# Turning the heads' outputs on VectorE, in 32x32 blocks, and parking them by four transfers

## The chip, the cores and the metric

The kernel runs on one core of a Trainium2 chip. The metric is the device time of one execution in microseconds (us), and it is measured in several runs. The engines of a core are named as in the profile: PE (TensorE's matmuls; PEld its weight loads), DVE (VectorE), ACT (ScalarE), POOL (GpSimd), SP (SyncE, which issues most of the transfers). L1268 is line 1268 of the kernel.

## The reference

One layer of a hybrid block: a normalised and modulated input goes through one projection, three groups of heads work on it, each output passes a gate, and one output projection adds it to the residual. The part that matters here is the normalisation of a head's output and its gate, cut from the reference:

```python
def from_heads(t):
    b, h, l, d = t.shape
    return t.transpose(0, 2, 1, 3).reshape(b, l, h * d)

def head_out(o, w, z):
    o = o * lax.rsqrt(jnp.mean(o * o, axis=-1, keepdims=True) + NORM_EPS) * w.astype(jnp.float32)
    return from_heads(o).astype(z.dtype) * jax.nn.silu(z)
...
    y_l = head_out(o_lf + flip_seq(o_lb), norm_w, z_l)
```

There are 512 latent tokens, a model width of 2048 and heads of 128: six gated-DeltaNet heads, six mLSTM heads, and 512 channels of long convolutions (Hyena).

## The kernel before

The input projection streams its weights in tiles of 128 x 512. Each is split into an upper and a lower half of the mantissa (`whi` by ACT, `wlo` by DVE, lines 275 and 276), and a product is three matmuls (lines 418, 419, 423; 421, 422, 425 for the context). That stream is the fill of the program: wherever nothing else is due, the next weight tiles stand.

Beside it run chains: the DeltaNet heads (`gdn`, one after another), the mLSTM scans (`ml_scans`), a row of gates, and four long convolutions (`convs`). A planner, `weave`, decides the order in which the program is written down: each chain yields a pair (cost on PE, latency), in units of its own, and is called again when its latency is over; the fill takes the rest. A list scheduler then fixes the order of instructions on each engine from that. The engines work in that order, and wait for each other by semaphores. A helper, `paced`, ties an instruction to the stream's matmul planned just before it (line 423), so that it does not run ahead.

A head ends in `head_norm` (line 1254, called 12 times). Its output `osb` has tokens on the partitions (4 pieces of 128 tokens) and the 128 channels of the head along each row. DVE takes the root mean square and scales it. Then `head_norm` yields a latency `LN` of 20, PE turns the four pieces by transposes into a PSUM bank (L1268), ACT copies the bank to the tile `yo` (L1270), and POOL issues one transfer of 256 KB (L1271) that parks it in `yraw` in DRAM, with channels as rows. `yo` has one buffer, shared with a tile of the heads' preparation (`qsq`, L1318) and one of the inversion.

The output projection is worked in four blocks of 512 columns. The first, `first_cols`, is the end of the fill. For each k of its 16 operands it calls `y_operand` (L1733): ACT issues the load of the gate `zt` (L1736), POOL that of the parked output `yr` (L1743), and DVE multiplies the two and the norm's weight (L1744; for four of the k's, the convolutions', L1741 does it without a parked output). The product is split into `yh` and `yl` (lines 275 and 276), and `y_product` makes the twelve matmuls (three by four tokens' pieces, L1762 to L1764). The long convolutions that are still to be done at that time share DVE, ACT, POOL and PE with it: four products `tt` with the spectrum `hs` (L1674 to L1677) in each of four frequency steps, two additions on POOL (L1679, L1680), the split `O`, and matmuls back (L323 to L325, and the ends, L1696 to L1700).

Of the kernel before, what the change touches and what calls it, by code (L numbers as in the profile page):

```python
# [10 lines left out]
F32 = mybir.dt.float32  # L11
# [3 lines left out]
AF = mybir.ActivationFunctionType  # L15
ALU = mybir.AluOpType
# [4 lines left out]
SEQ = 512  # L21
# [4 lines left out]
NL = SEQ // 128  # L26
# [3 lines left out]
EPS = 1e-6  # L30
# [194 lines left out]
def block_kernel(ctx: ExitStack, tc: tile.TileContext, io, out, dbg=None):  # L225
    nc = tc.nc
    PE, ACT, DVE, POOL, SP = nc.tensor, nc.scalar, nc.vector, nc.gpsimd, nc.sync
# [12 lines left out]
    def bank(tag, bufs, name=None):  # L240
        return ps.tile([128, 512], F32, tag=tag, bufs=bufs, name=name or tag)
# [26 lines left out]
    ident = const.tile([128, 128], F32, name="ident")  # L268
# [127 lines left out]
    yraw = dr.tile([KT, 128, SEQ], F32, name="yraw")  # L396
# [7 lines left out]
    def paced(ins):  # L404


        if stream[0] is not None:
            together(ins, [stream[0]])
# [51 lines left out]
    with ExitStack() as st:  # L460
# [23 lines left out]
        for k in range(KT):  # L484
# [11 lines left out]
            t = x_slot(F32)  # L496
# [27 lines left out]
        p = p_s()  # L524
        PE.matmul(p, w1, featsT, start=True, stop=True)
        h1 = sin_layer(p, 0)
        p = p_s()
# [86 lines left out]
        for k in range(KT):  # L614
# [6 lines left out]
            with tc.high_priority():  # L621
                for g in range(4):
                    G_ = slice(32 * g, 32 * g + 32)
                    i = PE.matmul(pa[G_], ones[:, 0:32], sqs[g], start=f, stop=l, tile_position=(0, 32 * g))
# [5 lines left out]
        pt = p_ml()  # L630
# [261 lines left out]
    with ExitStack() as st:  # L892
# [17 lines left out]
        for t0, n in ((0, 4), (4, 2)):  # L910
            pt = p_s()
# [339 lines left out]
        DVE.tensor_copy(MF[1][B, :, A], pv[B])  # L1251
        yield 1.0, LL

    def head_norm(o_sb, eps_ap, eps_imm, ss, kt_out, bank):

        v = s1.tile([128, NL], F32, tag="hn_v", bufs=2, name="hn_v")
        if eps_ap is not None:
            DVE.scalar_tensor_tensor(out=v, in0=ss, scalar=1.0 / 128, in1=eps_ap, op0=ALU.mult, op1=ALU.add)
        else:
            DVE.tensor_scalar(out=v, in0=ss, scalar1=1.0 / 128, scalar2=eps_imm, op0=ALU.mult, op1=ALU.add)  # L1260
        r = s1.tile([128, NL], F32, tag="hn_r", bufs=2, name="hn_r")
        rsqrt(s1, r, v, [128, NL], "rsq", 4)
        for t in range(NL):
            DVE.tensor_single_scalar(out=o_sb[:, t], in_=o_sb[:, t], scalar=r[:, t:t + 1], op=ALU.mult)
        yield 0, LN
        pt = bank()
        for t in range(NL):
            PE.transpose(pt[:, 128 * t:128 * t + 128], o_sb[:, t], ident)  # L1268
        yo = s1.tile([128, SEQ], F32, tag="yo", bufs=1, name="yo")
        ACT.activation(out=yo, in_=pt, func=AF.Copy)  # L1270
        POOL.dma_start(out=yraw[kt_out], in_=yo)  # L1271
        yield 0.6, 0.0

    def gdn_prep(h, kT, vT, qT):

# [91 lines left out]
    def gdn_scan(h, kT, qT, kt, vr, dd, eq, AT, MF):  # L1367
# [53 lines left out]
            S = s  # L1421
        if h == 0:
            dump("o_gdn", o_sb.rearrange("p t c -> p (t c)"))
        yield from head_norm(o_sb, eq, None, ss, h, p_st)

    def z_tile(k):

# [36 lines left out]
    def ml_scan(h, kT, vT, qT, oT):  # L1464
# [82 lines left out]
        junk = s1.tile([128, 128], F32, tag="junk", bufs=1, name="junk")  # L1547
        for j in range(NL):
            ACT.activation(out=junk, in_=o_sb[:, j], func=AF.Square, accum_out=ss[:, j:j + 1])
        yield from head_norm(o_sb, None, 4.0 * EPS, ss, 10 + h, p_s)  # L1550

    def residual_gate():

# [179 lines left out]
    def y_operand(k, pool):  # L1733

        zt = yt[0].tile([128, SEQ], F32, tag="zt", bufs=2, name="zt3")
        ACT.dma_start(out=zt, in_=zd[k])  # L1736
        w = hnw[:, 0:1] if k < 6 else hnw[:, 2:3] if k < 10 else hnw[:, 1:2]
        yr = yt[0].tile([128, SEQ], F32, tag="yr", bufs=2, name="yr3")
        if 6 <= k < 10:
            assert (1, (k - 6) // 2) in hdone  # L1740
            DVE.scalar_tensor_tensor(out=yr, in0=yv[k - 6], scalar=w, in1=zt, op0=ALU.mult, op1=ALU.mult)  # L1741
        else:
            POOL.dma_start(out=yr, in_=yraw[k])  # L1743
            DVE.scalar_tensor_tensor(out=yr, in0=yr, scalar=w, in1=zt, op0=ALU.mult, op1=ALU.mult)  # L1744
        yh[k] = pool.tile([128, SEQ], F32R, tag="y", bufs=KT, name="yh")
        yl[k] = pool.tile([128, SEQ], F32R, tag="y", bufs=KT, name="yl")
        split_hi_lo(yh[k], yl[k], yr)
# [124 lines left out]
```

## Time and profile before

| | us |
|---|---|
| median of three runs | 1501.56 (1501.19 to 1502.5) |
| profiled execution, own time | 1500.16 |
| its span | 1498.4 |
| PE busy | 1450.9 (97%) |
| DVE busy | 1033.0 (69%) |
| ACT busy | 572.6 (38%) |
| POOL busy | 217.0 (14%) |

The profiled execution is one execution; the span runs from its first instruction to its last. The busy times of engines overlap. PE's mean clock was 0.997 of full speed. A group of instructions is those of one line, engine and form of tile; its idle time is what the engine waited just before them.

### The profile page before, as it was taken

How to read it: one execution, taken by the hardware profiler on the slowest of the kernel's cores; microseconds unless marked ns; L12 is line 12 of the kernel's file. 1: busy time of each engine (PE TensorE's matmuls, PEld its weight loads, DVE VectorE, ACT ScalarE, POOL GpSimd, SP SyncE). 2: the span in 40 equal slices, each digit the busy share in tenths (PEclk: the TensorE clock that was granted, in tenths of full speed). 3: DMA queues.
4: the chain of work that ended last, by engine and by line, in shares of the span. 5: the costliest groups of instructions: out<-in, count | busy, mean ns of one | idle time of the engine just before them, and what ended most of it. 6: DMA issues, size and time to landing. Idle time of an engine off the chain costs nothing.

```text
span 1498.4 us, 25081 instructions
## 1 busy us (share of the span) xinstructions
PE 1450.9 (97%) x8822; PEld 1187.8 (79%) x8822; DVE 1033.0 (69%) x2685; ACT 572.6 (38%) x1367; POOL 217.0 (14%) x412
## 2 busy tenths in 40 slices
PE   5999999999999999999999999999999999999997
PEld 1566678888888888878887888888878888888785
DVE  4666777577868787867776776677675676774553
ACT  5443344425242524262435333533353333333431
POOL 2224002111110211021102101200011121210000
PEclk9999999999999999999999999999999999999999
DMA  9998623333244323442344223311322542465543
GB/s 316 318 320 289 224 74 106 95 105 114 85 138 117 120 93 117 127 125 92 120 117 132 85 71 93 114 57 57 86 79 81 166 169 92 143 231 154 163 129 102
DMA packets 145237, 202.82 MB, mean 135 GB/s; under 512 B 57222, under 2 KB 57703, under 8 KB 144856
## 3 DMA queue, kind: packets, MB, share of 16 engines
q1 hardware_dynamic: 89752, 159.50, 33.0%
q0 software_dynamic: 10048, 32.52, 6.9%
q10 hardware_dynamic: 45312, 9.21, 3.2%
q8 instruction: 69, 1.13, 0.3%
q14 instruction: 56, 0.46, 0.1%
HBM read 182.92 MB, written 18.26 MB: 134 GB/s over the span
## 4 chain that ended last, share of the span: by engine, by line
PE 80%; DVE 7%; DMA 5%; issue 3%; ACT 2%; POOL 1%; SPq 0%; ACTq 0%; DVEq 0%; POOLq 0%
PE ml L418 14%; PE ml L419 13%; PE ml L423 13%; PE mc L422 3%; PE mc L421 3%; PE mc L425 3%; PE st L317 2%; DVE wlo L276 2%; PE st L1764 1%; PE st L1763 1%; PE st L1762 1%; PE st L1386 1%; PE st L1395 1%; PE st L1379 1%; PE st L1508 1%
## 5 line engine op out<-in xcount | busy, mean ns | idle before, releaser
L418 PE MATMUL ml<-xh,whi 128*128 128x512 f32 x1024 | 423.1, 413 | 0.0
L419 PE MATMUL ml<-xs,whi 128*128 128x512 f32 x1024 | 407.1, 398 | 0.0
L423 PE MATMUL ml<-xh,wlo 128*128 128x512 f32 x1024 | 404.5, 395 | 0.0
L275 ACT ACTIVATE whi<-raw 128x512 fp32r<-128x512 f32 x320 | 200.9, 629 | 488.3 <-PE mc L422 165.4
L276 DVE TENSOR_TENSOR wlo<-raw,whi 128x512 fp32r<-128x512 f32 x320 | 222.2, 696 | 175.9 <-ACT whi L275 171.8
L418 PEld LDWEIGHTS ml<-xh,whi 128*128 128x128 f32 x1024 | 193.4, 189 | 33.8 <-issue 1.7
L423 PEld LDWEIGHTS ml<-xh,wlo 128*128 128x128 f32 x1024 | 192.7, 188 | 24.9
L419 PEld LDWEIGHTS ml<-xs,whi 128*128 128x128 f32 x1024 | 193.6, 189 | 18.9
L421 PE MATMUL mc<-cs,whi 128*128 128x256 f32 x384 | 110.4, 288 | 0.0
L422 PE MATMUL mc<-cs,whi 128*128 128x256 f32 x384 | 108.7, 283 | 0.0
L425 PE MATMUL mc<-cs,wlo 128*128 128x256 f32 x384 | 107.8, 281 | 0.0
L422 PEld LDWEIGHTS mc<-cs,whi 128*128 128x128 f32 x384 | 72.3, 188 | 16.0
L421 PEld LDWEIGHTS mc<-cs,whi 128*128 128x128 f32 x384 | 72.1, 188 | 15.6
L425 PEld LDWEIGHTS mc<-cs,wlo 128*128 128x128 f32 x384 | 73.4, 191 | 0.0
L1564 DVE SCALAR_TENSOR_TENSOR gacc<-mg,scol,gacc 128x512 f32<-128x512 f32 x60 | 45.0, 749 | 25.7 <-DMA mg<-in_mg_dram 17.4
L1281 POOL DMA_DIRECT2D G<-rows_d x36 | 19.8, 553 | 223.0 <-DVE T L1147 76.0
L1271 POOL DMA_DIRECT2D yraw<-yo x12 | 7.1, 589 | 293.2 <-ACT yo L1270 218.1
L1506 POOL TENSOR_SCALAR ke<-kt,wend 128x128 f32<-128x128 f32 x60 | 27.0, 452 | 87.5 <-PE st L1508 43.9
L1333 ACT ACTIVATE ex<-G,ngc 128x128 f32<-128x128 f32 x72 | 26.8, 397 | 32.4 <-DVE M L1335 10.9
L1763 PE MATMUL st<-wlo,yh 128*128 128x512 f32 x96 | 37.7, 392 | 0.0
L1764 PE MATMUL st<-whi,yl 128*128 128x512 f32 x96 | 37.7, 392 | 0.0
L1762 PE MATMUL st<-whi,yh 128*128 128x512 f32 x96 | 37.6, 391 | 0.0
(501 smaller groups left out, 2877.4 us busy)
## 6 DMA issues: line engine op xcount, KB each, us to landing
raw<-in_wt_dram SPq DMA_DIRECT2D x256, 256.0 KB, 2.8
mw<-in_mw_dram SPq DMA_DIRECT2D x128, 256.0 KB, 5.9
mg<-in_mg_dram SPq DMA_DIRECT2D x64, 256.0 KB, 2.7
raw<-in_wo_dram SPq DMA_DIRECT2D x64, 256.0 KB, 2.9
fraw<-in_wf_dram SPq DMA_DIRECT2D x16, 320.0 KB, 5.4
G<-rows_d POOLq DMA_DIRECT2D x36, 128.0 KB, 3.3
xs<-in_xT_dram SPq DMA_DIRECT2D x16, 256.0 KB, 5.9
hspec<-hv POOLq DMA_DIRECT2D x16, 256.0 KB, 5.7
```

The lines of the kernel that those rows point to most:

```text
L275: ACT.activation(out=hi, in_=src, func=AF.Copy)
L276: DVE.tensor_tensor(out=lo, in0=src, in1=hi.bitcast(F32), op=ALU.subtract)
L418: PE.matmul(pl[:m], wh, xh[:, kk], start=f, stop=False)
L419: PE.matmul(pl[:m], wh, xl[kk], start=False, stop=False)
L421: PE.matmul(pc[:m, :CTX], wh, ch[kk], start=f, stop=False)
L422: PE.matmul(pc[:m, :CTX], wh, cl[kk], start=False, stop=False)
L423: stream[0] = PE.matmul(pl[:m], wl, xh[:, kk], start=False, stop=l)
L425: PE.matmul(pc[:m, :CTX], wl, ch[kk], start=False, stop=l)
L1564: paced(DVE.scalar_tensor_tensor(out=acc, in0=m, scalar=sk, in1=acc, op0=ALU.mult, op1=ALU.add))
L1762: PE.matmul(o, yh[k][:, ts_], wh, start=f, stop=False)
L1763: PE.matmul(o, yh[k][:, ts_], wl, start=False, stop=False)
L1764: PE.matmul(o, yl[k][:, ts_], wh, start=False, stop=l)
```

## The change

`head_norm` no longer takes a bank. In place of the transposes, the copy and the one transfer, DVE turns the output in square blocks of 32 x 32, in one instruction, from `osb` to `yo`, which is now laid out as 128 partitions x 4 x 4 x 32. The blocks themselves stay where they were; so four transfers, issued by ACT and each `paced`, move 32 partitions (64 KB) each to their place in `yraw`, in runs of 512 bytes. The chain yields a cost of 0 and a latency of 2.5 after the turning and 0 at the end, where it yielded 0.6 after the transposes.

Within a row of `yraw` the tokens now stand in another order, by blocks. `y_operand` loads the parked output into a new tile, `pk`, with one buffer, and makes the product in four instructions of 128 columns, each of which reads its blocks from `pk` by strides and writes `yr` in the old order. The load is still POOL's.

```diff
-    def head_norm(o_sb, eps_ap, eps_imm, ss, kt_out, bank):
+    def head_norm(o_sb, eps_ap, eps_imm, ss, kt_out):
...
         yield 0, LN
-        pt = bank()
-        for t in range(NL):
-            PE.transpose(pt[:, 128 * t:128 * t + 128], o_sb[:, t], ident)
-        yo = s1.tile([128, SEQ], F32, tag="yo", bufs=1, name="yo")
-        ACT.activation(out=yo, in_=pt, func=AF.Copy)
-        POOL.dma_start(out=yraw[kt_out], in_=yo)
-        yield 0.6, 0.0
+        yo = s1.tile([128, 4, NL, 32], F32, tag="yo", bufs=1, name="yo")
+        DVE.transpose(out=yo.rearrange("p g t j -> p t g j"), in_=o_sb.rearrange("p t (g j) -> p t g j", j=32))
+        yield 0, 2.5
+
+        for q, Q in enumerate(QS):
+            paced(ACT.dma_start(out=yraw[kt_out].rearrange("(a i) (q x) -> q i a x", a=4, q=4)[q],
+                                in_=yo[Q].rearrange("i a t j -> i a (t j)")))
+        yield 0, 0.0
...
         else:
-            POOL.dma_start(out=yr, in_=yraw[k])
-            DVE.scalar_tensor_tensor(out=yr, in0=yr, scalar=w, in1=zt, op0=ALU.mult, op1=ALU.mult)
+            pk = yt[0].tile([128, SEQ], F32, tag="pk", bufs=1, name="pk")
+            POOL.dma_start(out=pk, in_=yraw[k])
+            for t in range(NL):
+                ts_ = slice(128 * t, 128 * t + 128)
+                DVE.scalar_tensor_tensor(out=yr[:, ts_].rearrange("p (q j) -> p q j", q=4), scalar=w, op0=ALU.mult,
+                                         op1=ALU.mult, in0=pk.rearrange("p (q t j) -> p t q j", t=NL, q=4)[:, t],
+                                         in1=zt[:, ts_].rearrange("p (q j) -> p q j", q=4))
```

The two calls of `head_norm` drop their last argument. Below L1266 a line of the kernel after stands one lower than before, and from L1745 on six lower.

What this does to the order of the engines is shown at three places. The first is DVE in the first columns of the output projection, at two frequency steps of a convolution: `tt` and `O` are the convolution's, `yr`, `yl` the gate's product and its lower half, `wlo` the lower half of a weight. Before:

```order
L276 TENSOR_TENSOR O<-tt,O 128x256
L1744 SCALAR_TENSOR_TENSOR yr_14716<-yr_14716,hnw,zt_14714 128x512
L276 TENSOR_TENSOR O<-tt,O 128x256
L276 TENSOR_TENSOR wlo<-raw,whi 128x512
L276 TENSOR_TENSOR yl<-yr_14716,yh 128x512
L1674 TENSOR_TENSOR tt<-st,hs 128x256
L1675 SCALAR_TENSOR_TENSOR tt<-st,c_alt,hs 128x256
L1676 TENSOR_TENSOR tt<-st,hs 128x256
L1677 SCALAR_TENSOR_TENSOR tt<-st,c_alt,hs 128x256
```

And after, in that stage:

```order
L276 TENSOR_TENSOR O<-tt,O 128x256
L1748 SCALAR_TENSOR_TENSOR yr_14441<-pk,hnw,zt_14439 128x128
L276 TENSOR_TENSOR wlo<-raw,whi 128x512
L276 TENSOR_TENSOR O<-tt,O 128x256
L1748 SCALAR_TENSOR_TENSOR yr_14441<-pk,hnw,zt_14439 128x128 x3
L1645 TENSOR_TENSOR eo<-hy 128x256
L1675 TENSOR_TENSOR tt<-st,hs 128x256
L1676 SCALAR_TENSOR_TENSOR tt<-st,c_alt,hs 128x256
L1677 TENSOR_TENSOR tt<-st,hs 128x256
L1678 SCALAR_TENSOR_TENSOR tt<-st,c_alt,hs 128x256
L276 TENSOR_TENSOR yl<-yr_14441,yh 128x512
```

One product has become four, spread around the convolution's work. `eo`, the first fold of a convolution, has moved into this place, since a second convolution now lies here; before, only the last did.

The second place is POOL in the same stage: loads of the parked outputs between additions of the convolution. Before:

```order
L1743 DMA yr_14716<-yraw 128x512
L1743 DMA yr_14767<-yraw 128x512
L1679 TENSOR_TENSOR tt<-tt 128x256
L1680 TENSOR_TENSOR tt<-tt 128x256
L1743 DMA yr_14827<-yraw 128x512
L1679 TENSOR_TENSOR tt<-tt 128x256
L1680 TENSOR_TENSOR tt<-tt 128x256
```

And after:

```order
L1745 DMA pk<-yraw 128x512
L1680 TENSOR_TENSOR tt<-tt 128x256
L1681 TENSOR_TENSOR tt<-tt 128x256
L1680 TENSOR_TENSOR tt<-tt 128x256
L1681 TENSOR_TENSOR tt<-tt 128x256
L1745 DMA pk<-yraw 128x512 x4
L1680 TENSOR_TENSOR tt<-tt 128x256
L1681 TENSOR_TENSOR tt<-tt 128x256
```

The four loads in a row go to the one buffer, each behind the products that read the one before, and they stand ahead of the next additions.

The third place is ACT at the end of a head: `yo` is the head's output, `whi` the upper half of a weight, `kT`, `tanh` and `qT` the next head's. Before:

```order
L1082 ACTIVATE tanh<-kT 128x256
L1270 ACTIVATE yo<-s 128x512
L275 ACTIVATE whi<-raw 128x512
L1082 ACTIVATE tanh<-kT 128x512
L275 ACTIVATE whi<-raw 128x512 x2
L1069 ACTIVATE qT<-ml,gcw 128x512
```

And after:

```order
L1082 ACTIVATE tanh<-kT 128x512
L1271 DMA yraw<-yo 32x4x128 x2
L275 ACTIVATE whi<-raw 128x512
L1271 DMA yraw<-yo 32x4x128 x2
L275 ACTIVATE whi<-raw 128x512
L1069 ACTIVATE qT<-ml,gcw 128x512
```

The copy has gone, and the four issues stand in pairs around a weight's half.

## Rows read from the trace of the kernel before

**Rows 1.** The page's first part (busy time of each engine, share of the span, instructions) and, from its fourth part, the chain that ended last by engine.

```profile
PE 1450.9 (97%) x8822; PEld 1187.8 (79%) x8822; DVE 1033.0 (69%) x2685; ACT 572.6 (38%) x1367; POOL 217.0 (14%) x412
...
PE 80%; DVE 7%; DMA 5%; issue 3%; ACT 2%; POOL 1%; SPq 0%; ACTq 0%; DVEq 0%; POOLq 0%
```

**Rows 2.** All instructions of line 1268 on PE, the transposes of the heads' outputs: engine, operation, names, count; shortest, median and longest in ns; first and last start.

```profile
L1268 PE MATMUL s<-ident,osb x24: 270/272/330, 376.9 to 1142.5; 128*128 128x128 f32 x24
...
L1268 PE MATMUL st<-ident,osb x24: 270/272/273, 417.2 to 1189.3; 128*128 128x128 f32 x24
```

**Rows 3.** The timeline of PE around the first head's transposes: start in us, duration in us, then line and names; the transposes share one row (x4).

```profile
376.63 0.39 PE L423 MATMUL ml<-xh,wlo 128*128 128x512 f32 x1
376.86 0.60 PE L1268 MATMUL s<-ident,osb 128*128 128x128 f32 x4
377.22 0.48 PE L418 MATMUL ml<-xh,whi 128*128 128x512 f32 x1
377.54 0.39 PE L419 MATMUL ml<-xs,whi 128*128 128x512 f32 x1
```

**Rows 4.** Groups of instructions by line and form on ACT and POOL, the last from the page: busy us and mean ns of one, then idle time ahead of them and what ended it. The weights' upper halves, the copies of the heads' outputs from PSUM, and the issues that park them.

```profile
L275 ACT ACTIVATE whi<-raw 128x512 fp32r<-128x512 f32 x320 | 200.9, 629 | 488.3 <-PE mc L422 165.4 <-PE ml L419 156.7 <-issue 30.2
...
L1270 ACT ACTIVATE yo<-st 128x512 f32<-128x512 f32 x6 | 3.6, 598 | 10.8 <-PE st L1268 10.8
...
L1270 ACT ACTIVATE yo<-s 128x512 f32<-128x512 f32 x6 | 3.5, 590 | 0.6 <-PE s L1268 0.5
...
L1271 POOL DMA_DIRECT2D yraw<-yo x12 | 7.1, 589 | 293.2 <-ACT yo L1270 218.1
```

**Rows 5.** Groups by line and form on DVE, columns as in rows 4: the gate's product, a product of a quarter of its size, and block transposes of two sizes.

```profile
L1744 DVE SCALAR_TENSOR_TENSOR yr<-yr,hnw,zt 128x512 f32<-128x512 f32 x12 | 8.9, 745 | 2.3 <-DMA yr<-yraw 2.3
...
L1534 DVE SCALAR_TENSOR_TENSOR osb<-nm,dn,osb 128x128 f32<-128x128 f32 x24 | 8.4, 351 | 0.8
...
L1184 DVE STREAM_TRANSPOSE L<-U 128x384 f32<-128x384 f32 x6 | 3.4, 571 | 0.2
...
L1101 DVE STREAM_TRANSPOSE Mb<-Mc 128x192 f32<-128x192 f32 x6 | 2.3, 378 | 0.6 <-ACT Mc L1099 0.4
```

**Rows 6.** Two stretches of the span: its length, then the busy time and count of instructions of PE, PEld, DVE, ACT and POOL, PE's granted clock, the DMA share and GB/s. The second is the stretch from the first products of the output columns to the end of the last convolution.

```profile
1200.00:1292.80 92.80, 91.69 (x537) 80.21 (x537) 68.33 (x138) 28.42 (x60) 18.53 (x24) 1.00 0.37 121
1292.80:1334.50 41.70, 40.68 (x221) 34.18 (x220) 34.19 (x64) 17.31 (x34) 12.19 (x19) 1.00 0.62 192
```

**Rows 7.** The timeline of DVE in that second stretch: start in us, duration in us, line and names, and in brackets the idle time ahead with what ended it.

```profile
1305.16 0.49 DVE L276 TENSOR_TENSOR O<-tt,O 128x256 fp32r<-128x256 f32 x1 [0.65 <-ACT O L275]
1305.58 0.74 DVE L1744 SCALAR_TENSOR_TENSOR yr<-yr,hnw,zt 128x512 f32<-128x512 f32 x1
1306.24 0.41 DVE L276 TENSOR_TENSOR O<-tt,O 128x256 fp32r<-128x256 f32 x1
1306.58 0.68 DVE L276 TENSOR_TENSOR wlo<-raw,whi 128x512 fp32r<-128x512 f32 x1
1307.18 0.68 DVE L276 TENSOR_TENSOR yl<-yr,yh 128x512 fp32r<-128x512 f32 x1
1307.78 0.41 DVE L1674 TENSOR_TENSOR tt<-st,hs 128x256 f32<-128x256 f32 x1
...
1308.84 0.47 DVE L1677 SCALAR_TENSOR_TENSOR tt<-st,c_alt,hs 128x256 f32<-128x256 f32 x1
...
1331.38 0.42 DVE L1696 TENSOR_TENSOR cv<-st,bs 128x256 f32<-128x256 f32 x1
...
1332.05 0.68 DVE L276 TENSOR_TENSOR wlo<-raw,whi 128x512 fp32r<-128x512 f32 x1
1332.65 0.74 DVE L1698 SCALAR_TENSOR_TENSOR cv<-hy,c_skip,cv 128x512 f32<-128x512 f32 x1
1333.31 0.68 DVE L276 TENSOR_TENSOR yl<-yr,yh 128x512 fp32r<-128x512 f32 x1
```

**Rows 8.** The timeline of PE, in the same stretch: five starts of the output columns' matmuls (512 wide) lie from the first row to the second, and eight of the convolution's (256 wide) from the second to the third.

```profile
1317.71 0.39 PE L1763 MATMUL ml<-wlo,yh 128*128 128x512 f32 x1
...
1318.86 0.28 PE L323 MATMUL st<-iv,O 128*128 128x256 f32 x1
...
1319.80 0.28 PE L325 MATMUL st<-iv,O 128*128 128x256 f32 x1
```

**Rows 9.** Issues of transfers: the z tiles on ACT, and the read-back of the parked outputs on POOL, each with its shortest, median and longest issue in ns, and the read-back's time to landing in us.

```profile
L1736 ACTq DMA_DIRECT2D zt<-zd x16: 326/327/350, 1168.6 to 1340.9; - x16
...
L1743 POOL DMA_DIRECT2D yr<-yraw x12: 538/555/597, 1159.2 to 1330.5; - x12
...
DMA to landing us min/median/max: 2.9/3.1/4.3
```

**Rows 10.** The waits of the whole span: who waited for whom; total us, times, longest us.

```profile
DVE O L276 <- ACT O L275: 9.2, 15, 1.1
...
PE s L1478 <- ACT kt L1479: 6.7, 4, 2.7
...
DVE tt L1674 <- DMA hs<-hspec: 2.5, 4, 1.0
```

**Rows 11.** Two stretches of the head stage, columns as in rows 6.

```profile
640.00:660.00 20.00, 17.62 (x103) 14.29 (x102) 12.26 (x34) 14.04 (x39) 7.79 (x16) 1.00 0.49 150
780.00:800.00 20.00, 17.51 (x85) 14.27 (x83) 15.14 (x27) 4.72 (x9) 1.90 (x4) 1.00 0.51 144
```

More of the change, by code (lines that the diff above doesn't have):

```diff
@@ L1423, in gdn_scan @@
             dump("o_gdn", o_sb.rearrange("p t c -> p (t c)"))
-        yield from head_norm(o_sb, eq, None, ss, h, p_st)
+        yield from head_norm(o_sb, eq, None, ss, h)
     def z_tile(k):
@@ L1549, in ml_scan @@
             ACT.activation(out=junk, in_=o_sb[:, j], func=AF.Square, accum_out=ss[:, j:j + 1])
-        yield from head_norm(o_sb, None, 4.0 * EPS, ss, 10 + h, p_s)
+        yield from head_norm(o_sb, None, 4.0 * EPS, ss, 10 + h)
     def residual_gate():
```

## The prediction

> **What bounds the kernel now.** I read the shares of the engines first, then the groups of the lines that the change touches, then the stage in which the gate's products are made. TensorE (PE) is busy for 1450.9 of 1498.4 us, and the chain that ended last is 80% PE, 7% VectorE (DVE), 5% DMA [rows 1]. So PE time that goes is time that goes, wherever PE is full; work added to DVE, ScalarE (ACT) or GpSimd (POOL) costs only where PE comes to wait for it. The place to look for that is the stretch in which the output projection's first columns run together with the last long convolution: there DVE is busy for 34.19 of 41.70 us while PE is still nearly full (40.68) [rows 6]. Just before, it is 68.33 of 92.80. That stretch is the only one, of those the change touches, where DVE and PE stand so close.
>
> **What goes from PE.** Each of the 12 heads' outputs has four transposes on PE, 48 in all, at 272 ns each [rows 2]. Their durations overlap, so the price is the gap they make in the stream: after the matmul of 376.63 the four start at 376.86, the next matmul at 377.22, and the one behind it not until 377.54 [rows 3]. From 376.63 to 377.54 are 0.91 us, for two steps that take 0.23 us each in a full stream (376.63 to 376.86, or 1.15 us for five [rows 8]): 0.91 - 0.46 = 0.45 us a head, 12 x 0.45 = 5.4 us. The bounds are 12 x 0.36 (only 376.86 to 377.22) = 4.3 and 48 x 0.272 = 13.1 us. I take 5.4, read from the place itself; nearly all of these heads lie where PE is full, so I count all of it as gain.
>
> A rule of the Trainium skill speaks against this part: "VectorE: DVE Perf Modes", section "Rules for kernel authors", says to make a 128x128 transpose on TensorE if a PSUM destination will do, and VectorE's only for 32x32 blocks. The row at 376.86 agrees that TensorE's is cheap, 0.45 us for four; by that rule the most that this part can give is the 5.4 us above.
>
> **What goes from and comes to the others in the head stage.** ACT loses 12 copies of 0.59 us = 7.1 us, POOL 12 issues of 0.59 us = 7.1 us [rows 4]. DVE gains 12 block transposes of 128x512. The trace has 571 ns for 128x384 and 378 ns for 128x192, 1.0 ns a column, so 0.70 us (bounds: 0.57, the wide row itself, and 1.1, twice that row) and 8.4 us in all [rows 5]. ACT gains 48 issues of transfers; its issues of the z tiles, which have the nearest row, take 0.327 us: 15.7 us [rows 9]. Neither is on the path by itself: ACT is busy 38% and DVE 69% of the span [rows 1], and PE's weight tiles hide it. If that cover were gone, the 8.4 us would come on top. Each issue is tied to the product planned just before it (the last matmul of a weight tile, line 423), so ACT waits there for PE; queued behind it are the rounding of the next weights' halves, for which DVE waits and then PE. The issues stand in ACT's order between the weight halves (two, a half, two more), so each pair holds a half up by 0.65 us, while ACT sat idle 488 us before these halves, 165 of it until PE [rows 4]: it is early, and I count the wait at nothing. What waits for the parked data is far behind: a head's output is read back only in the last stage.
>
> What may change in the head stage is how a head's end collides with its neighbours. PE loses time there in some 20-us windows: the two worst show 17.62 and 17.51 us busy of 20 [rows 11]; the wait for the copies of the mLSTM's keys makes 6.7 us of it [rows 10]. The change keeps the chain of heads waiting for longer (a planner cost of 2.5 in place of 0.6), so heads, scans and fill interleave anew, and ACT's order of those copies against the inversion's load changes for heads 2 to 5. I take 0 for it, between -6.7 (all of those waits go) and +5 (two more such windows).
>
> **The gate's product.** The one product of 128x512 (745 ns) is split in four of 128x128; the nearest row of that size is 351 ns [rows 5]. By start to start, the large one is 0.66 us (1305.58 to 1306.24 [rows 7]); the difference of the durations is 394 ns, so a small one starts 0.66 - 0.39 = 0.27 us behind the last. Four are 1.08 us, 0.42 us more for each k. Bounds: 0 (the elements are as many) and 4 x 0.351 - 0.745 = 0.66 us. Twelve k's give 5.0 us more on DVE, ten of them, 4.2 us, in the busy stretch.
>
> The Trainium skill says in "Perfetto Trace Analysis", section "Optimizing Scalar/DVE Operations", that each instruction pays a fixed access overhead and that small ones should be joined where the engine is saturated; the rows agree in direction, 351 ns for a quarter of the elements of a 745 ns one.
>
> The order adds more to that stretch. The convolution (1,0) used to run inside the input projection's tiles; now both (1,0) and (1,1) lie among the first 132 matmuls of the output columns, with ten k's. Counted in the new order of DVE, from the first yl of that stage to the end of the last convolution, by start-to-start times of [rows 7]: 13 yl and 11 wlo at 0.60 = 14.4; 40 small products at 0.27 = 10.8; 2 large ones at 0.66 = 1.3; 8 frequency steps, four tt each (1.46) = 11.7; 16 O at 0.38 = 6.1; 4 folds at 0.34 = 1.4; 2 el at 0.60 = 1.2; 4 ends of a convolution (0.67 + 0.66 + 0.60) = 7.7. Sum 54.6 us. PE in the same stretch: 192 convolution matmuls at 0.1175 (0.94 us for eight [rows 8]) = 22.6, 16 small transposes at 0.11 (0.45 for four, above) = 1.8, 132 output matmuls at 0.23 = 30.4. Sum 54.8 us. So DVE alone would just do. But it also waits:
> - for ACT's rounding of O, 9.2 us in 15 waits [rows 10], 0.61 us in each of 8 steps = 4.9;
> - for the spectra (hs), 2.5 us in 4 waits [rows 10], 0.6 each, 4 loads = 2.4;
> - for the new single buffer pk. A load can start only when the fourth product has read the last one, and takes 0.55 us of issue and 3.1 us to land [rows 9], 3.65 us. Nine reloads fall in the stretch; DVE has 2 to 4 us of other work between two of them, so about half wait 1 to 1.8 us, 5 to 6 in all. Part of that lies where it would wait for O anyway: I take 4 (0 to 10).
>
> That is 54.6 + 4.9 + 2.4 + 4.0 = 65.9 us against PE's 54.8. The last end of a convolution (1.9) need not be over for PE to go on: 64.0 - 54.8 = 9.2. Of that, 1.0 us is lost already before (41.70 - 40.68 [rows 6]). New stall: 8.2 us, with 2 to 15 as its ends (waits absorbed, or all nine reloads in full). What follows is PE-bound, so nothing gives it back.
>
> Sum: -5.4 + 0 + 8.2 = +2.8 us on the profiled execution's 1500.16 us, 1503.0 us. The span is 1498.4, so 1.8 us lie around it and stay. The profiled execution is 1.4 us below the median of the runs, 1501.56: the forecast on the median is 1504.4 us, or 1504.
>
> **Rivals.**
> 1. DVE's spare time takes it all up. In the old stretch DVE was at 82% [rows 6], waited 2.5 us for hs, and PE lost 1.0 us; the waits may go on lying beside work of PE, with matmuls of ready k's queued, and the planner's fill gives PE other columns. Against it: the count of DVE's work now equals PE's. Then only the 5.4 us remain: 1496.2 us.
> 2. The single buffer pk becomes a serial loop, slower: each of nine reloads costs its whole 3.65 us of turnaround less the 1.7 us that lies next to it, and POOL, which issues these loads in order with the additions of tt, holds those back behind a load that waits. Four loads stand there in a row ahead of an addition. It decides from the point at which DVE's work between two loads is under 3.65 us. 9 x 1.95 = 17.5 in place of the 4: 13.5 more would be 1518; with the half of it beside O's waits, 1511 us. Against it: two of the loads are issued long before.
> 3. The collisions in the head stage dissolve, because the scan's copies now stand ahead of the inversion's load: -6.7, and 1504.4 - 6.7 = 1497.7 us. For it speaks the new order of ACT; against it, that the copies then meet something else.
> That the parking does not do what it says (four transfers with runs of 512 bytes instead of one with 2 KB) is no rival of its own: nothing waits for it near.
>
> **How the numbers follow.** Forecast 0.45 (own range 1499 to 1509), rival 1 0.24, rival 2 0.17, rival 3 0.14. About 0.2% is what a measurement of this kernel can tell from no change: 1498.6 to 1504.6 us. Faster: 0.07 of the forecast, 0.85 of rival 1, half of rival 3 = 0.03 + 0.20 + 0.07 = 0.30. Same: half of the forecast, 0.15 of rival 1, 0.45 of rival 3 and a little of rival 2 = 0.34. Slower: the rest, 0.36. The time is that of the forecast, 1504; the range reaches from just below rival 1 to just above rival 2, 1495.5 to 1512.
>
> **What the changed profile would show.** No transposes in line 1268's place on PE, and PE's busy sum lower by 5 us or more; 12 block transposes on DVE of about 0.70 us; 48 products of 128x128 near 0.35 us. In the stretch with both convolutions: DVE above 90%, waits of DVE for pk of about 1 us several times, PE idle 7 to 10 us before lines 1768 to 1770 and the convolution's matmuls. Wrong would be: PE full in that stretch (then rival 1); waits for pk of over 2 us nearly each time (rival 2); PE idle in the head windows below 3 us in sum (rival 3); or block transposes of 1.1 us or more, by which DVE would delay weight halves in the head stage, which no term here holds.

## The result, and the profile after

The kernel after takes 1520.18 us (median of five runs, 1516.77 to 1523.32) against 1502.5 us: a ratio of 1.0121, with a 95% interval of 1.0104 to 1.0138. That is 18 us slower; the forecast was 2.8 us slower, with a range that ended at 1512. Put beside the kernel before a second time, on another occasion, the ratio was 1.0100 (1.0078 to 1.0121). Left out throughout are three executions in a slow state, of 1689, 2879 and 7409 us.

The profiled execution took 1520.18 us with a span of 1518.4, 20.0 us more than the span before. Where these 20 us lie shows in three views. First the busy times of the page, which answer to [rows 1]:

```profile
PE 1455.9 (96%) x8774; PEld 1189.9 (78%) x8774; DVE 1042.5 (69%) x2733; ACT 569.4 (38%) x1355; POOL 215.8 (14%) x400
```

PE has lost 48 transposes, 5.4 us by the forecast's price, and is still busy for 5.0 us more. Idle, it is 62.5 us in place of 47.5. Next, the same three stretches of the span in both kernels, columns as in [rows 6]: up to the first head's end, the head stage, and the rest without the tail. Before:

```profile
0.00:370.00 370.00, 346.46 (x2077) 253.42 (x2078) 246.15 (x644) 157.98 (x351) 75.05 (x134) 1.00 0.61 197
370.00:1200.00 830.00, 820.46 (x5341) 698.35 (x5340) 601.78 (x1679) 316.94 (x826) 110.74 (x234) 1.00 0.35 104
1200.00:1475.00 275.00, 271.37 (x1355) 226.25 (x1355) 176.18 (x332) 93.60 (x182) 31.25 (x44) 1.00 0.48 152
```

After:

```profile
0.00:370.00 370.00, 346.00 (x2045) 252.80 (x2046) 246.47 (x644) 157.38 (x350) 74.97 (x134) 0.99 0.60 196
370.00:1200.00 830.00, 816.02 (x5294) 694.08 (x5294) 596.64 (x1672) 310.64 (x812) 101.98 (x213) 0.99 0.34 100
1200.00:1475.00 275.00, 261.35 (x1301) 217.12 (x1300) 182.55 (x362) 93.17 (x177) 38.84 (x53) 0.99 0.48 155
```

In the head stage PE idles for 14.0 us (830 - 816.02) where it idled for 9.5. In the last stretch it idles for 13.7 us (275 - 261.35) where it idled for 3.6. The first stretch, which holds of the changed instructions only the first block transpose (368.5 us), has the same idle time within 0.5 us. So 14.5 us of the 20 are new pauses of PE, in two places.

The rest is in the clock. PE's busy time should have fallen by 5.4 and rose by 5.0: some 10 us of it is matmuls at the lower clock. Here is one pause of PE and what follows, in windows of 1 us, of the kernel after (columns as in [rows 6]; the number behind the five engines is PE's granted clock):

```profile
1426.00:1427.00 1.00, 0.41 (x2) 0.00 (x0) 0.00 (x0) 0.22 (x1) 0.00 (x0) 1.00 0.71 246
1427.00:1428.00 1.00, 0.00 (x0) 0.00 (x0) 0.56 (x1) 0.91 (x2) 0.00 (x0) 1.00 0.07 27
1428.00:1429.00 1.00, 0.60 (x2) 0.28 (x2) 0.82 (x2) 0.31 (x2) 0.00 (x0) 1.00 0.02 6
1429.00:1430.00 1.00, 1.00 (x5) 0.84 (x6) 0.52 (x1) 0.45 (x1) 0.00 (x0) 1.00 0.68 252
1430.00:1431.00 1.00, 1.00 (x4) 0.77 (x3) 0.17 (x1) 0.01 (x1) 0.00 (x0) 0.55 0.72 215
1431.00:1432.00 1.00, 1.00 (x4) 0.77 (x3) 0.35 (x1) 0.73 (x2) 0.00 (x0) 0.50 0.77 197
1432.00:1433.00 1.00, 1.00 (x4) 0.81 (x3) 0.79 (x2) 0.52 (x1) 0.00 (x0) 0.50 0.32 123
1433.00:1434.00 1.00, 1.00 (x4) 0.78 (x4) 0.35 (x2) 0.63 (x1) 0.00 (x0) 0.75 0.45 100
```

PE stops at 1426.4 and starts again at 1428.2, 1.77 us later by its timeline, with another gap of 0.23 us behind the first matmul. The pause waits for a weight tile that landed late (ACT stood idle for 2.79 us until it did), not for a changed line. From about 1430.1 on, with PE full again, the granted clock is 0.50 (1.2 GHz, where it had been 2.4) for 3.4 us, and that costs 0.45 + 0.50 + 0.50 + 0.25 = 1.7 us of matmuls. The profile of the kernel after has six such falls, one of them nearly twice as long, which cost 11.2 us together; that of the kernel before has one, of 1.5 us. Two of the six, 3.4 us, lie ahead of the first head, where the two kernels run the same work, so they are not the change's. Not every pause brings a fall: of eleven pauses of 1.4 us or more between 40 and 1475 us in the profile after, six did, and the pause that ends at 47 us, 1.75 us long in both kernels, was followed by one in the kernel after and by none in the kernel before.

The two profiles differ more in this than the runs do. Over the five runs of the kernel after the mean granted clock was 0.992, over 23 runs of the kernel before on the second occasion 0.995. Those 0.003 of some 1456 us are 4 to 5 us, about a quarter of what the change costs.

The changed instructions themselves, groups by line and form on DVE, and then the issues on ACT (shortest, median, longest ns):

```profile
L1748 DVE SCALAR_TENSOR_TENSOR yr<-pk,hnw,zt 128x128 f32<-128x128 f32 x48 | 14.7, 346 | 7.0 <-DMA pk<-yraw 7.0
...
L1267 DVE STREAM_TRANSPOSE yo<-osb 128x512 f32<-128x512 f32 x12 | 8.5, 711 | 0.3
```

```profile
L1271 ACTq DMA_DIRECT2D yraw<-yo x48: 309/452/682, 381.0 to 1219.7; - x48
```

A block transpose is 711 ns (forecast 0.70), a small product 346 ns (0.35), an issue 452 ns (0.33). The waits of PE behind 370 us (total us, times, longest):

```profile
PE s L1491 <- DVE PT L1495: 6.4, 3, 2.6
PE s L1479 <- ACT kt L1480: 5.0, 3, 1.9
PE st L323 <- ACT O L275: 4.9, 3, 2.1
PE ml L1768 <- ACT yh L275: 3.0, 6, 0.7
```

Before, PE waited 6.7 us for the copies `kt` in the head stage [rows 10]. Now a wait for `PT`, DVE's product in the mLSTM scan, has come beside it (before, one of 1.0 us), and in the last stretch PE waits for `O` and `yh`, which both come after work that stands behind the gate's products on DVE.

### The profile page after: what moved, and what is told of

It is laid out like the page before. It is cut to its first block, busy times and chain, and to the rows that moved or that the text cites. A ratio compares the mean times of both kernels' runs of the same rounds, so it can differ in the third digit from the quotient of the medians.

```text
span 1518.4 us, 25057 instructions
## 1 busy us (share of the span) xinstructions
PE 1455.9 (96%) x8774; PEld 1189.9 (78%) x8774; DVE 1042.5 (69%) x2733; ACT 569.4 (38%) x1355; POOL 215.8 (14%) x400
## 5 line engine op out<-in xcount | busy, mean ns | idle before, releaser
L1394 POOL TENSOR_SCALAR ke<-kt,kend 128x128 f32<-128x128 f32 x60 | 24.9, 419 | 254.6 <-PE st L1396 241.5
L1507 POOL TENSOR_SCALAR ke<-kt,wend 128x128 f32<-128x128 f32 x60 | 30.8, 518 | 68.7 <-PE st L1509 37.0
```

## The experiments

The kernel after differs from the one before in four things that can be had one by one: the head's end (turning on DVE, four transfers), the gate's product in four instructions, the single buffer `pk`, and the planner's figures (a latency of 2.5 in place of a cost of 0.6). Times are given as ratios to the kernel before with their intervals; a thousandth is 1.5 us.

### The planner's figures alone, and all but them

```diff
-        yield 0.6, 0.0
+        yield 0, 2.5
+        yield 0, 0.0
```

> The kernel before with only the planner's figures of the change: the chain of a head yields a latency of 2.5 after its end in place of a cost of 0.6. TensorE still turns, ScalarE still copies, one transfer parks, the gate's product is one instruction. By its order two convolutions again lie among the first 132 matmuls of the output columns. Theory P (the moved convolution and the new interleaving of heads cost the time): 10 to 16 us slower than before, with PE idle 6 us or more in the last 300 us. Theory G (the single buffer pk and the four small products cost it): within 3 us of before. Theory C (the granted clock, which falls to half for some 3 us behind a pause of PE, holds about half of the loss): every such fall more than before's one costs about 1.7 us, whatever made the pause; three or more of them if P is right.

Measured: 1.0040 (1.0024 to 1.0055), 6.0 us slower. Theory P was half right: no work was added, and a third of the loss is there. Of theory C the falls are there: the profile has four ahead of the tail, one of them nearly twice as long, where before's has one. But one of the four lies ahead of the first head, and over the runs the mean clock was 0.9935 against 0.9947, which is under 2 us, so that the clock holds half of the loss is not borne out. The reverse, with the planner's figures of before in the kernel after:

```diff
-        yield 0, 2.5
...
-        yield 0, 0.0
+        yield 0.6, 0.0
```

> The kernel after with the planner's figures of before (no latency of 2.5 behind the block transpose, a cost of 0.6 at the end); blocks, four transfers, pk and the four products stay. One convolution lies in the first 81 matmuls of the output columns, as before. Theory P: 2 to 6 us faster than before (the 5.4 us of the transposes less something for the gate), so 18 to 25 us faster than after. Theory G: 5 to 12 us slower than before. Theory C: the mean granted clock is back at 0.996 or more if the pauses are gone.

Measured: 1.0037 (1.0021 to 1.0053), 5.6 us slower. So theory G holds as well: with the planner as before the blocks still lose. The profiled execution was at a clock of 0.997, and the ten runs at the 0.995 of the kernel before, though the pauses of the last stretch were not gone.

### The gate alone, and all but the gate

```diff
-            POOL.dma_start(out=yr, in_=yraw[k])
-            DVE.scalar_tensor_tensor(out=yr, in0=yr, scalar=w, in1=zt, op0=ALU.mult, op1=ALU.mult)
+            pk = yt[0].tile([128, SEQ], F32, tag="pk", bufs=1, name="pk")
+            POOL.dma_start(out=pk, in_=yraw[k])
+            for t in range(NL):
+                ts_ = slice(128 * t, 128 * t + 128)
+                DVE.scalar_tensor_tensor(out=yr[:, ts_].rearrange("p (q j) -> p q j", q=4), scalar=w, op0=ALU.mult,
+                                         op1=ALU.mult, in0=pk[:, ts_].rearrange("p (q j) -> p q j", q=4),
+                                         in1=zt[:, ts_].rearrange("p (q j) -> p q j", q=4))
```

> The kernel before with only the gate of the change: the parked output goes to pk (one buffer) and is multiplied in four instructions of 128 columns, read in the natural order since the parking is that of before. Theory P: 0 to 3 us slower than before. Theory G: 6 to 12 us slower, with waits of VectorE for pk of 5 us or more in sum.

Measured: 1.0076 (1.0054 to 1.0098), 11.4 us slower, with one convolution in the stage as before: theory G. Here one sees why. Three timelines of the kernel with the gate alone, DVE, POOL and PE (of PE only the starts behind a pause), after the last convolution:

```profile
1339.45 1.14 DVE L1747 SCALAR_TENSOR_TENSOR yr<-pk,hnw,zt 128x128 f32<-128x128 f32 x4 [0.22 <-DMA pk<-yraw]
1340.50 0.69 DVE L276 TENSOR_TENSOR wlo<-raw,whi 128x512 fp32r<-128x512 f32 x1
1341.28 0.69 DVE L276 TENSOR_TENSOR yl<-yr,yh 128x512 fp32r<-128x512 f32 x1
1344.28 1.14 DVE L1747 SCALAR_TENSOR_TENSOR yr<-pk,hnw,zt 128x128 f32<-128x128 f32 x4 [2.30 <-DMA pk<-yraw]
1345.33 0.68 DVE L276 TENSOR_TENSOR wlo<-raw,whi 128x512 fp32r<-128x512 f32 x1
1346.11 0.69 DVE L276 TENSOR_TENSOR yl<-yr,yh 128x512 fp32r<-128x512 f32 x1
1349.06 1.14 DVE L1747 SCALAR_TENSOR_TENSOR yr<-pk,hnw,zt 128x128 f32<-128x128 f32 x4 [2.26 <-DMA pk<-yraw]
```

```profile
1340.88 0.54 POOL L1744 DMA_DIRECT2D pk<-yraw  x1 [4.07 <-DVE yr L1747]
1345.71 0.54 POOL L1744 DMA_DIRECT2D pk<-yraw  x1 [4.29 <-DVE yr L1747]
```

```profile
1341.30 0.50 PE L1767 MATMUL ml<-whi,yh 128*128 128x512 f32 x1 [1.59 <-ACT yh L275]
...
1346.13 0.49 PE L1767 MATMUL ml<-whi,yh 128*128 128x512 f32 x1 [1.82 <-ACT yh L275]
```

The four products run from 1339.45 to 1340.50; only then may POOL issue the next load (1340.88), and it lands for 1344.28. A turn, from one load's products to the next load's, is 4.8 us, twice in a row. PE needs twelve matmuls for one k, at 0.228 us from start to start there 12 x 0.228 = 2.74 us, and so it pauses at each k: 1.59 and 1.82 us here, 1.75 and 2.23 us at the next two. In sum DVE waits for 8.9 us for `pk` in this kernel, and PE, which waits for `yh` behind the products, for 10.8 us, where the kernel before has one such wait, of 0.7 us:

```profile
DVE yr L1747 <- DMA pk<-yraw: 8.9, 5, 2.7
...
PE ml L1767 <- ACT yh L275: 10.8, 10, 2.2
```

The other half, the kernel after with the gate of before (the first `-` lines above put back), leaves the blocks' order as it is:

> The kernel after with the gate of before: one product of 128x512 and two buffers, which leaves out the putting back of the blocks' order, so the tokens of these rows stand in another order. The planner's figures are those of the change. Theory P: 8 to 15 us slower than before. Theory G: 0 to 5 us faster than before.

Measured: 1.0022 (1.0007 to 1.0038), 3.3 us slower, in neither theory's range. With the planner's 6.0 and the head's part (-4.5, below) this should be 1.5; the intervals allow it.

### One buffer or four instructions

> The kernel after with the planner's figures of before and a second buffer for pk; the four products stay. Theory L (the loop of the one buffer: four products, issue, landing, 4.8 us a turn against 2.74 us that PE needs for one k) has the waits of VectorE for pk under 2 us in sum, PE idle 3 to 6 us behind 1200 us in place of the 13.8 of one buffer, and the time 8 to 11 us below that of one buffer, so 2 to 6 us faster than before. Theory S (the four small products themselves load VectorE too much) has PE idle still 10 us or more there and the time 3 to 8 us above before.

```diff
-            pk = yt[0].tile([128, SEQ], F32, tag="pk", bufs=1, name="pk")
+            pk = yt[0].tile([128, SEQ], F32, tag="pk", bufs=2, name="pk")
```

Measured: 0.9992 (0.9980 to 1.0003), 1.2 us faster or nothing. Against the same kernel with one buffer that is 6.8 us (some 4 to 10 by the two intervals), and no wait for `pk` of more than 0.3 us is left. The last stretch of the two kernels, first with one buffer, then with two:

```profile
1200.00:1475.00 275.00, 261.22 (x1294) 216.64 (x1293) 175.23 (x347) 90.81 (x178) 29.91 (x42) 0.99 0.44 139
```

```profile
1200.00:1475.00 275.00, 267.24 (x1329) 222.50 (x1328) 178.17 (x361) 92.45 (x181) 29.42 (x42) 0.99 0.45 143
```

PE idles for 13.8 and for 7.8 us. Theory L had it right in kind, though it asked for 8 to 11 us; the last few us belong to the other theory, as the next kernel shows:

```diff
+            for t in range(NL):
+                ts_ = slice(128 * t, 128 * t + 128)
-            DVE.scalar_tensor_tensor(out=yr, in0=yr, scalar=w, in1=zt, op0=ALU.mult, op1=ALU.mult)
+                DVE.scalar_tensor_tensor(out=yr[:, ts_], in0=yr[:, ts_], scalar=w, in1=zt[:, ts_], op0=ALU.mult, op1=ALU.mult)
```

> The kernel before with the gate's product in four instructions of 128 columns, in place in yr, which keeps its two buffers. Theory L: within 2 us of before. Theory S: 5 to 12 us slower.

Measured: 1.0023 (1.0011 to 1.0036), 3.5 us slower, between the two theories. Four instructions in place of one cost this by themselves, with the old buffers. The rule on small instructions of the Trainium skill ("Perfetto Trace Analysis", "Optimizing Scalar/DVE Operations"), which the forecast weighed, agrees: four times 345 ns stand against 745 ns for the same elements.

### The head's part alone

The kernel after with the planner's figures and the gate of before:

> The head's part alone, with the planner's figures of before: block transposes and four transfers, and the gate of before, which leaves out the putting back of the blocks' order (the tokens of these rows stand in another order). If the transposes' 0.45 us a head is a gain in full, 4 to 7 us faster than before, with PE idle as before. If the four issues on ScalarE or VectorE's 0.71 us a head come back as new waits, within 2 us of before. If the granted clock decides, it follows the count of its falls, 1.7 us each, against before's.

Measured: 0.9970 (0.9956 to 0.9984), 4.5 us faster. PE idles in the head stage for 11.0 us (830 - 819.05), 1.4 more than before, and in the last stretch for 5.8, 2.2 more:

```profile
370.00:1200.00 830.00, 819.05 (x5323) 696.97 (x5322) 608.09 (x1695) 312.27 (x817) 103.12 (x223) 1.00 0.36 106
1200.00:1475.00 275.00, 269.22 (x1340) 224.07 (x1339) 175.24 (x331) 92.33 (x181) 30.47 (x43) 1.00 0.46 144
```

So DVE's 0.71 us and ACT's four issues a head are nearly hidden, and the transposes' price of 0.45 us a head is close to what comes back, 4.5 of 5.4 us; the interval of the runs, 2.4 to 6.6 us, does not tell how close.

### A second try at the kernel after, and its second buffer

> The kernel after itself, beside the two below. If its parts add up as measured one by one (head -4.5, product in four +3.4, one buffer +6.8, planner's figures +6 to +8 us), 12 to 14 us slower than before. If they make each other worse, 16 to 20 us slower, as in the first comparison.

> The kernel after with a second buffer for pk and nothing else changed. If the parts add up, 5 to 7 us slower than before, so 7 us below after. If the moved convolution makes the one buffer worse, the second gives back more: 9 to 12 us below after. If under the moved convolution it is VectorE's load and no longer the buffer that decides, less than 4 us below after.

Measured on one occasion: after 1.0100 (1.0078 to 1.0121), 15.0 us slower, between the two ranges; with two buffers 1.0030 (1.0015 to 1.0044). The second buffer gives back 10.5 us (some 7 to 14 by the intervals). That is more than the 6.8 with the planner as before, but the two intervals overlap, so that the buffer costs more here is likely and not shown. The order has a reason for it. Here are DVE and POOL of the kernel after, in the convolution's frequency steps:

```profile
1331.02 0.87 DVE L1748 SCALAR_TENSOR_TENSOR yr<-pk,hnw,zt 128x128 f32<-128x128 f32 x3
...
1333.26 0.39 DVE L1748 SCALAR_TENSOR_TENSOR yr<-pk,hnw,zt 128x128 f32<-128x128 f32 x1
...
1338.84 0.61 DVE L1748 SCALAR_TENSOR_TENSOR yr<-pk,hnw,zt 128x128 f32<-128x128 f32 x2 [2.77 <-DMA pk<-yraw]
```

```profile
1333.48 0.77 POOL L1681 TENSOR_TENSOR tt<-tt 128x256 f32<-128x256 f32 x1
1334.19 0.56 POOL L1745 DMA_DIRECT2D pk<-yraw  x1
1340.34 0.71 POOL L1680 TENSOR_TENSOR tt<-tt 128x256 f32<-128x256 f32 x1 [5.59 <-DVE tt L1676]
```

Of one k's four products, three run at 1331.02 and the last at 1333.26, with the convolution's products between: the buffer is held for 2.6 us where the four together take 1.1. The load behind it then stands in POOL's order after two additions, starts at 1334.19, and DVE, in order, waits 2.77 us for it, with the next frequency step's products and so POOL's next additions (1340.34) behind; PE, which needs the `O` of that step, then waits for it for 2.1 us, the longest of its waits for `O` in the table of waits above. With two buffers the parts add up as measured singly: -4.5 + 3.5 + 6.0 = 5.0 us against 4.5.

### What in the planner's figures costs it

Two things move by them: the convolution (1,0) comes into the last stage, and heads and scans meet elsewhere. The first alone, the kernel before with

```diff
-            yield lambda: n in hready and clock[0] >= hready[n]
+            yield lambda: n in hready and clock[0] >= hready[n] + (16 if n == 10 else 0)
```

> The kernel before, with the third convolution (1,0) held back by 16 of the planner's units and nothing else changed: it lies, as in the kernel after, among the first 132 matmuls of the output columns (60 of them ahead of its end), while the heads keep their places of before. If the moved convolution makes the planner's part of the loss, 5 to 8 us slower than before, with PE idle 6 us or more behind 1200 us and 9 to 10 us between 370 and 1200 us. If the heads' new places do, within 2 us of before.

Measured: 1.0009 (0.9995 to 1.0023): most likely 1.4 us, not told from none. By subtraction some 4.6 us of the planner's 6.0 (1 to 8 by the intervals) are in the heads' places. Head stage and last stretch, first with the planner's figures, then with the moved convolution alone:

```profile
370.00:1200.00 830.00, 816.11 (x5303) 693.89 (x5303) 586.35 (x1640) 314.57 (x816) 108.35 (x225) 0.99 0.33 99
1200.00:1475.00 275.00, 269.22 (x1368) 225.61 (x1367) 186.69 (x357) 97.19 (x190) 39.40 (x53) 1.00 0.50 161
```

```profile
370.00:1200.00 830.00, 820.13 (x5323) 697.70 (x5320) 599.40 (x1673) 315.52 (x824) 107.41 (x230) 0.99 0.34 101
1200.00:1475.00 275.00, 268.05 (x1354) 224.19 (x1353) 178.40 (x327) 93.83 (x182) 35.00 (x49) 1.00 0.48 155
```

PE idles in the head stage for 13.9 us in the first, 9.9 in the second (before: 9.5). In the last stretch both have somewhat more than before, 5.8 and 7.0 against 3.6, of which the runs of the second show 1.4 us as time; its profile is that of the slowest of its ten runs (1509.23 us, median 1505.21). What PE waits for in the head stage with the planner's figures:

```profile
PE s L1491 <- DVE PT L1495: 6.0, 3, 3.4
PE s L1479 <- ACT kt L1480: 5.6, 4, 2.1
```

One of the three waits for `PT`, the longest, begins on ACT; here are its timeline and PE's start:

```profile
813.76 0.31 ACTq L1177 DMA_DIRECT2D ublk<-R  x1
...
814.77 0.63 ACT L275 ACTIVATE whi<-raw 128x512 fp32r<-128x512 f32 x1 [5.83 <-issue]
815.31 0.68 ACT L1494 ACTIVATE ex<-mrow,am 128x128 f32<-128x128 f32 x2
```

```profile
816.96 0.80 PE L1491 MATMUL s<-qT,kT 128*128 128x128 f32 x2 [3.38 <-DVE PT L1495]
```

`ublk<-R` is a transfer at the end of a DeltaNet head's inversion; ACT reaches it early (its last work before ends at 808.9) and is held there until the inversion's last product on DVE is done (813.72). Behind it, in ACT's order, stand a weight's half and the exponentials `ex` of the mLSTM scan (815.31), which `PT` and then PE (816.96) wait for: a pause of 3.38 us. The kernel after has the same pause, 2.56 us, at 813.14. Before, the scan met the inversion at its copies `kt` instead, behind the load `U<-ublk` (a pause of 2.7 us [rows 10]); now it meets it at two places. This is read from the timelines for the longest wait alone; no run takes that wait away by itself. Which of the two figures it is:

```diff
-        yield 0.6, 0.0
+        yield 0, 0.0
```

> The kernel before with a cost of 0 in place of 0.6 at a head's end and no latency: by its order neither the convolution nor the scans' copies move against the weight tiles. If it is the latency of 2.5 that makes the planner's part, within 2 us of before. If the lower cost does, 4 to 8 us slower.

Measured: 0.9985 (0.9971 to 1.0000): no loss, perhaps a small gain. The kernel with the planner's figures differs from this one by the latency alone, so it is the latency.

### Three ways to a faster kernel

All have the head's part and the planner's figures of before, and restore the blocks' order without four products on DVE. The read-back in four loads of short runs:

```diff
-            POOL.dma_start(out=yr, in_=yraw[k])
+            for q in range(4):
+                POOL.dma_start(out=yr.rearrange("p (t q j) -> q p t j", t=NL, q=4)[q],
+                               in_=yraw[k].rearrange("p (q t j) -> q p t j", t=NL, q=4)[q])
```

> The head's part with the planner's figures of before, and the order put back by the read-back itself: four loads of 64 KB for each k in place of one of 256 KB, in runs of 128 bytes on chip, then one product of 128x512 from two buffers. Theory L: no turn of one buffer is left, so as the head's part alone, 2 to 6 us faster than before, if GpSimd's four issues (2.2 us a k) stay under PE's 2.74 us. Against it: the issues stand ahead of GpSimd's additions for the convolution, and short runs land late: PE idle 5 us or more more than before, and 3 to 10 us slower.

Measured: 1.0044 (1.0026 to 1.0063), 6.6 us slower. All the loads on POOL, issue in ns and time to landing in us:

```profile
L1743 POOL DMA_DIRECT2D yr<-yraw x48: 749/752/819, 1156.8 to 1338.7; - x48
...
DMA to landing us min/median/max: 2.5/3.2/4.4
```

An issue takes 0.75 us where the plain one took 0.555 [rows 9], so four are 3.0 us, above PE's 2.74 us for a k, and DVE waits 9.0 us for `yr` in six waits. Whether the issues or the two buffers of `yr` do this, this run does not tell. A copy on ACT into the right order, with two buffers for `pk`:

```diff
+            ACT.activation(out=yr.rearrange("p (t q j) -> p t q j", t=NL, q=4),
+                           in_=pk.rearrange("p (q t j) -> p t q j", t=NL, q=4), func=AF.Copy)
+            DVE.scalar_tensor_tensor(out=yr, in0=yr, scalar=w, in1=zt, op0=ALU.mult, op1=ALU.mult)
```

> The head's part with the planner's figures of before and two buffers for pk; ScalarE puts the blocks back in order with one copy of 128x512 (about 0.65 us a k), and VectorE's product is one instruction again. If it was the four instructions on VectorE that kept the version with two buffers from the head's part alone, 3 to 5 us faster than before. If ScalarE's copy stands in the way of the weights' halves and of yh, within 2 us of before or slower.

Measured: 0.9993 (0.9981 to 1.0005). And four loads a k, two on POOL and two on ACT, to `pk` with two buffers:

```diff
+            pk = yt[0].tile([128, SEQ], F32, tag="pk", bufs=2, name="pk")
+            for q in range(4):
+                (ACT if q % 2 else POOL).dma_start(out=pk.rearrange("p (t q j) -> q p t j", t=NL, q=4)[q],
+                               in_=yraw[k].rearrange("p (q t j) -> q p t j", t=NL, q=4)[q])
+            DVE.scalar_tensor_tensor(out=yr, in0=pk, scalar=w, in1=zt, op0=ALU.mult, op1=ALU.mult)
```

> A candidate: the head's part with the planner's figures of before; the read-back puts the blocks in order by four loads a k, two issued by GpSimd and two by ScalarE, into pk with two buffers, and one product of 128x512 goes from pk to yr. If it was the two yr buffers, each held by load, product and split in turn, that made the four loads late in the earlier version, it is 2 to 5 us faster than before. If the short runs or the issues themselves are late, VectorE waits for pk 5 us or more in sum and it is no faster than before, and if ScalarE's queue is held by its issues, slower by 3 us or more.

Measured: 1.0002 (0.9989 to 1.0015). DVE waits only 0.4 us for `pk`, so the loads are no longer late, and still the time is that of the kernel before. None of the three beats it; with the blocks put back, by whichever engine, the head's 4.5 us are spent again. Two buffers with four products, ACT's copy and the loads on two queues end within 1.5 us of each other; PE idles in their last stretches for 7.8, 9.2 and 8.1 us, where the head's part alone has 5.8. What makes each of these was not followed further.

## Why the prediction was wrong

Two steps failed in the main: what the single buffer costs, taken as 4 us, and what the new order does in the head stage, taken as 0. The clock, for which there was no term, adds to both.

- **What goes from PE.** Right: 5.4 us forecast, 4.5 us measured (2.4 to 6.6) for the head's part with all that it adds.
- **The head stage's collisions, taken as 0 between -6.7 and +5.** This step failed: the planner's figures cost 6.0 us, with the moved convolution's 1.4 in it some 4.6 for the heads' places, at the upper end of the bound. The forecast saw that the order changes and took the middle for want of a reason. What it could have read is what then stood where: in ACT's new order the scan's exponentials come behind a transfer that waits for the inversion.
- **The second convolution in the stage.** The step "DVE alone would just do", by which the moved convolution made the stall, failed: moved alone it costs 1.4 us, not told from none, and the gate alone costs 11.4 us without it. The forecast's stall of 8.2 us is near the 10.0 us by which PE's idle time grew in the last stretch, but that is in part luck. In the stretch that it was worked out for, from the first `yl` (1290.07) to the end of the last convolution (1358.3), PE idles for 5.4 us, not 7 to 10, and DVE is busy for 85%, not over 90%; the rest lies ahead of it and behind it.
- **The product in four.** 4.2 us of DVE's time were counted in the stage, 3.5 us came out as time, though not by the sum in which they stood.
- **The single buffer, taken as 4 us (0 to 10).** This is the term that was sized wrong most: 6.8 to 7.9 us (from the pairs with one buffer and two, and with one buffer and none but the four products) with the planner as before, and 10.5 with the planner of the change, each within some 4 us. The turn was forecast well, 3.65 us and the products' 1.08; measured 4.8. But the forecast set DVE's sum against PE's over the whole stretch, 54.6 against 54.8, and said that DVE has 2 to 4 us of other work between two loads. That is an average. Behind the convolution the k's come one after another, DVE has 1.2 us of other work (`wlo` and `yl`), and PE wants a k every 2.74 us. Rival 2 named this mechanism, the serial loop and the loads that hold POOL's additions back, and gave it 0.17 and 1511 us. Its own sign, waits for `pk` of over 2 us nearly each time, is there with the gate alone, behind the convolution (2.30 and 2.26 us); in the kernel after it is one wait of six.
- **The clock.** No term held it. A pause of about 2 us of PE can be followed by some 3 us at half clock, and a row of before had shown it, the window behind the pause at 800 us, at a mean clock of 0.92:

```profile
800.00:820.00 20.00, 19.74 (x155) 16.70 (x156) 13.19 (x41) 13.81 (x43) 8.44 (x16) 0.92 0.47 145
```

It was not priced. In the pair of profiles it is 10 us of 20, of which 3.4 lie ahead of the change and are chance; over the runs it is 4 to 5 us. The experiments' times hold their own share of it already.

The terms, -4.5 + 3.5 + 10.5 + 6.0, make 15.5 us; the kernel after was 15.0 us slower on one occasion and 18.2 on the other. This is less of a check than it looks, since the 10.5 is itself taken from the kernel after. With 6.8 in its place, the buffer's price with the planner as before, the sum is 11.8, and 3 to 6 us are left for noise and for what the parts do to each other.

## What to carry to other kernels

A buffer that is loaded, read and loaded again in turn has a period of its own; set that period against what the bottleneck needs for one item at the place where items come fastest, not the sums of the stage. A planner's figure that moves no work by itself can still cost more than the work that is saved, when two chains then meet in the order of an engine that works in order. And a pause of PE can cost more than its length: 1.7 us more here, in matmuls at 1.2 GHz, behind some pauses and not behind others like them.

## What the runs showed of the hardware

A pause of PE of 1.8 us was followed, 1.9 us after PE's restart, by 3.4 us at a granted clock of 0.50, at a cost of 1.7 us. Not each pause was: PE idled for 2.56 us until 813.14 us in the kernel after and the clock stayed at 1.00, while in a second profile of the same kernel 2.08 us at that place were followed by a fall. DVE's block transposes of 32 x 32 in fp32 took 711 ns for 128x512, 11 ns above the line of the two smaller sizes [rows 5]. An issue of a load in runs of 128 bytes took POOL 0.75 us against 0.555 us for a plain one; ACT's issues of the parking transfers, in runs of 512 bytes, took 0.45 us (median; 0.31 to 0.68) against 0.33 for the z tiles.
